# The low halves of the second layer's weights: a negated copy on ScalarE and an adding DMA in place of a subtraction

## The chip, the cores and the metric

One core of a Trainium2 chip runs the kernel. The metric is the device time of one execution in microseconds (us). Names of engines as in the profile: PE is the matrix engine (PEld its weight loads, which overlap it), DVE is VectorE, ACT is ScalarE, POOL is GpSimd, SP is the queue that issues DMAs.

## The reference, cut to what matters

Two layers over 640 tokens (128 prompt tokens and 512 latent tokens), width 1024. Layer 0 is gated attention, layer 1 a bidirectional state-space scan (SSD). The change touches only the two weight matrices of layer 1:

```
proj = h @ w_in            # layer 1: (640 x 1024) @ (1024 x 5184)
z, xbc, dt = split(proj)
xbc = silu(conv3(xbc));  xs, bs, cs = split(xbc)
dt = softplus(dt + bias)
y_f, h_f = scan(xs * dt_f, a_f * dt_f, bs, cs, h0_f)     # chunks of 128 tokens
y_b, h_b = the same, backwards
y = rms_norm((y_f + y_b + d_skip * xs) * silu(z), gnorm_w)
out = x + gate * (y @ w_out)                             # (640 x 2048) @ (2048 x 1024)
```

## The kernel before

**Split operands.** Every large product is computed from fp32 values that are split into a high part (rounded to the reduced type fp32r) and a low part, the value minus its high part. PE then makes three products: high times high, high times low, low times high. A weight tile so exists three times in SBUF: `raw` (as loaded), `wh` (high) and `wl` (low).

**How weights arrive.** `load_split` does it in halves: SP issues the DMA of a raw half (512 KB), ACT copies it to `wh` (line 73, the rounding is the copy's output type), and DVE or POOL subtracts, `wl = raw - wh` (line 74). Which of the two subtracts is set by the list `self.weng`, which is rotated at each half: POOL alone at the start of layer 1, then DVE, POOL, POOL in turn, then DVE alone from the first weights of `w_out` on. All three tiles come from the pool `w`, which has two buffers for each name. So a raw half can be issued when the raw half two places ahead has been read, and a load (two halves) can write its `wh` and `wl` when PE is done with the load two places ahead.

**Stages of layer 1.** (1) 21 loads from `w_in`: 16 of 256 columns for x and z, 4 of 2 x 128 columns for the B and C of a group, and one of 64 columns for dt (a single half of 256 KB). A load of 256 columns serves two units; a unit is 48 matmuls of 322 columns (line 914; lines 1073 for the first z). Between them stand, for each of 4 groups, the scan's steps: POOL masks two decay tiles (lines 1116, 1117) that SP has loaded (line 1112), ACT exponentiates them (1121), POOL adds them (1122), DVE multiplies (1128), PE makes the products. (2) 16 loads from `w_out`, each two rows of 128 of the inner dimension: first 8 for token tiles 2 and 3 (`part_mm`, 24 matmuls of 512 columns a load), the first ones between the steps of the last group's scan, then the same 8 again for token tiles 1, 4 and 0 (36 matmuls a load; line 1368). The output follows at once.

**Order.** Each engine works through its own list in order. A scheduler that builds the kernel decides the order within an engine by a simulated timeline, so an edit can move rows on every engine.

Of the kernel before, what the change touches and what calls it, by code (L numbers as in the profile page):

```python
# [11 lines left out]
ALU = mybir.AluOpType  # L12
# [27 lines left out]
def r32(ap):  # L40
    return ap.bitcast(F32)
# [12 lines left out]
class Hybrid:  # L54
    def __init__(self, tc, A, O, tap=None):
        self.tc, self.nc, self.A, self.O = tc, tc.nc, A, O
        self.tap = tap or {}
        self.n = 0

    def nm(self, s):  # L60
# [15 lines left out]
    def load_split(self, wp, hi, lo, src):  # L76
        k, w = hi.shape[1], hi.shape[2]
        step = max(1, 1024 // w)
        for k0 in range(0, k, step):
            ks = slice(k0, min(k, k0 + step))  # L80
            raw = self.tl(wp, [P, step, w], tag="raw")
            rv = raw[:, 0:ks.stop - k0, :]
            self.nc.sync.dma_start(out=rv, in_=src[:, ks, :])
            self.weng = self.weng[1:] + self.weng[:1]
            self.split(hi[:, ks, :], lo[:, ks, :], rv, self.weng[0])

# [923 lines left out]
    def layer1(self, hT, wp, pj, pa, ctx):  # L1010
        nc, tc, A, O = self.nc, self.tc, self.A, self.O
        sp = self.pool("s1", ctx=ctx)
        self.weng = [nc.gpsimd]
        wk = self.pool("s2", bufs=2, ctx=ctx)
        self.fss = self.tl(self.cp, [P, NT], tag="fss")
        self.one = self.tl(self.cp, [P, 1], tag="one")
# [168 lines left out]
        def lag(f, g, j, before=None):  # L1185
            u = wcur.get("u")
            f(g, j)
            v = wcur["u"]
            if before:
                wcur["u"] = u  # L1190
                before[0](*before[1:])
                wcur["u"] = v
# [8 lines left out]
            self.y_turn(t, g, wk, "u")  # L1201

        def part_mm(k0):
            self.weng = [nc.vector]
            w = self.load_wide(wp, A["l1_w_out"], k0)
            for t in (2, 3):
                if k0 == 0:
                    ps = self.tl(pj, [P, 1024], tag="pj")
                    self.PS[t] = [ps[:, 0:512], ps[:, 512:1024]]
                self.out_mm(t, w, k0)  # L1210
# [7 lines left out]
        next(gen, None)  # L1218
        lag(x_unit, 0, 2, (x_turn, 0, 1))
        next(gen, None)  # L1220
        self.weng = [nc.vector, nc.gpsimd, nc.gpsimd]
        lag(x_unit, 0, 3, (x_turn, 0, 2))
        lag(bc_unit, 0, 0, (x_turn, 0, 3))
        lag(bc_unit, 0, 1, (b_turn, 0))
# [3 lines left out]
        for g in range(NG):  # L1228
# [3 lines left out]
            if last:  # L1232
                pt_ = lambda t, k: (lambda: part_turn(t, k))
                pm_ = lambda k: (lambda: part_mm(k))
                fl = {0: [zf(0), zf(1)], 1: [zf(2)], 2: [zf(3), pt_(2, 0), pt_(3, 0)], 3: [pt_(2, 1), pt_(3, 1), pm_(0)],
                      4: [pt_(2, 2), pt_(3, 2), pm_(2)], 5: [pm_(4)], 6: [pm_(6)], 7: [pm_(8)], 8: [pm_(10)]}
            else:
                fl = {j: [nx(j)] for j in range(4)}
                fl.update({4: ([zf(0)] if g else []) + [lambda: x_turn(g + 1, 3)], 5: [zf(1)] if g else [], 6: [lambda: bc_unit(g + 1, 0)], 7: [lambda: bc_unit(g + 1, 1)], 8: [zf(2), lambda: b_turn(g + 1)], 9: [zf(3)]})
# [59 lines left out]
        for n in range(4, 6):  # L1299
            self.mod_gate(1, n, self.grow[1, n], pa, "a", wk, "xw0", "xw0", 2)  # L1300
        part_mm(12)
        part_mm(14)
        for t in (2, 3):
            self.final_out(t, wk, "u", "ym")
# [160 lines left out]
```

## Time and profile before

| what | value |
|---|---|
| median of 3 runs | 996.82 us (993.96 to 996.9) |
| the profiled execution | 996.55 us, its span 994.8 us |
| granted clock of PE over the span | 0.981 |
| busy: PE, DVE, ACT, POOL | 937.9, 656.3, 515.3, 431.1 us |
| layer 1 begins at about | 430 us of the span |
| DMA: moved, share of the 16 engines | 127.91 MB, 39.6% |

The span is that of the instructions; 1.75 us of the profiled time lie around it. Matmuls overlap, so a PE that is busy for all of a stretch is not at its peak by that alone. A figure in brackets behind a row of the timeline is the engine's idle time ahead of it and what ended it.

### The profile page before, as it was taken

What the parts mean: (1) busy time and instruction counts of PE and PEld (TensorE: products, weight loads), DVE (VectorE), ACT (ScalarE), POOL (GpSimd) and SP (SyncE); (2) the same over time, 40 slices, a digit from 0 to 9 for tenths busy, and PEclk for the clock granted to TensorE, in tenths of its full rate; (3) what the DMA queues carried; (4) which work ended last, traced back from release to release, by engine and by line L of the source; (5) the groups of instructions that cost most, each with busy time, mean ns of one, the idle gap of its engine ahead of it and who ended that gap; (6) DMA issues with size and microseconds to landing.
All of it is one profiled execution on the core that took longest, in us unless ns stands there. A gap on an engine that the chain in (4) does not pass through costs nothing. (4 is left out here: it accounts for less than half of the span.)

```text
span 994.8 us, 17000 instructions
## 1 busy us (share of the span) xinstructions
PE 937.9 (94%) x6466; PEld 835.0 (84%) x6466; DVE 656.3 (66%) x1046; ACT 515.3 (52%) x1212; POOL 431.1 (43%) x415
## 2 busy tenths in 40 slices
PE   5998999999999989989899979999999999989998
PEld 3897879879997789989898878889988898658786
DVE  5468665666675764884759854956587547797663
ACT  5355666757775763433446564446436642554240
POOL 3345235227270162364267475739484853333000
PEclk9999999999999989999999999999999999989999
DMA  9942234221113222333234352344524441455752
GB/s 319 351 128 87 86 127 138 67 73 43 37 49 107 85 93 100 123 106 89 86 131 148 121 181 88 109 139 145 151 87 146 156 133 64 128 183 190 257 194 96
DMA packets 90354, 127.91 MB, mean 129 GB/s; under 512 B 6816, under 2 KB 65312, under 8 KB 90272
## 3 DMA queue, kind: packets, MB, share of 16 engines
q1 hardware_dynamic: 90272, 126.82, 39.6%
q8 instruction: 51, 0.84, 0.3%
q14 instruction: 31, 0.25, 0.1%
HBM read 115.10 MB, written 11.70 MB: 127 GB/s over the span
## 5 line engine op out<-in xcount | busy, mean ns | idle before, releaser
L914 PE MATMUL pj<-h,wh 128*128 128x322 f32 (+1 forms) x1248 | 298.3, 325 | 8.7 <-DVE B L999 7.5
L914 PEld LDWEIGHTS pj<-h,wh 128*128 128x128 f32 (+1 forms) x1248 | 211.2, 189 | 21.5 <-issue 14.0
L74 POOL TENSOR_TENSOR wl<-raw,wh 128x512 fp32r<-128x512 f32 (+1 forms) x70 | 133.1, 1912 | 184.6 <-ACT wh L73 182.9
L914 PE MATMUL pj<-h,wl 128*128 128x322 f32 (+1 forms) x624 | 198.6, 319 | 0.0
L73 ACT CAST wh<-raw 128x1024 fp32r<-128x1024 f32 (+1 forms) x117 | 103.0, 912 | 79.7 <-DMA raw<-in_l_w_out 22.4
L1121 ACT ACTIVATE am<-am,nb 128x128 f32<-128x128 f32 x320 | 97.9, 389 | 62.4 <-POOL am L1117 39.9
L914 PEld LDWEIGHTS pj<-h,wl 128*128 128x128 f32 (+1 forms) x624 | 118.2, 190 | 3.9 <-issue 3.6
L283 PE MATMUL pp<-wh,big 128*128 128x256 f32 x576 | 112.1, 284 | 0.5 <-ACT sg L527 0.5
L283 PEld LDWEIGHTS pp<-wh,big 128*128 128x128 f32 x576 | 91.2, 188 | 0.9 <-ACT sg L527 0.7
L74 DVE TENSOR_TENSOR wl<-raw,wh 128x1024 fp32r<-128x1024 f32 x47 | 62.8, 1347 | 38.0 <-ACT wh L73 38.0
L283 PE MATMUL pp<-wl,big 128*128 128x256 f32 x288 | 81.1, 282 | 0.0
L74 DVE TENSOR_TENSOR pl<-pt,ph 128x512 fp32r<-128x512 f32 (+1 forms) x100 | 59.2, 599 | 25.9 <-ACT ph L73 25.1
L633 DVE TENSOR_REDUCE nm<-S 128x1 f32<-128x640 f32 x64 | 52.3, 819 | 13.7 <-PE S L630 12.7
L73 ACT CAST ph<-pt 128x512 fp32r<-128x512 f32 (+1 forms) x100 | 51.4, 517 | 19.1 <-PE pt L658 14.3
L1122 POOL TENSOR_TENSOR am<-am,am 128x1024 f32<-128x1024 f32 x20 | 48.7, 2437 | 26.2 <-ACT am L1121 26.2
L637 ACT ACTIVATE Pt<-S,nm 128x640 f32<-128x640 f32 x64 | 51.2, 802 | 13.4 <-PE pt L658 9.9
L1368 PE MATMUL pj<-wh,h 128*128 128x512 f32 x160 | 54.4, 413 | 0.5 <-ACT wh L73 0.5
L283 PEld LDWEIGHTS pp<-wl,big 128*128 128x128 f32 x288 | 54.3, 188 | 0.0
L658 PE MATMUL pt<-cst,Pt 128*128 128x128 f32 x320 | 51.6, 279 | 2.6 <-DVE pl L74 2.3
L630 PE MATMUL S<-kT,qT 128*128 128x320 f32 x256 | 51.1, 324 | 2.3 <-ACT Pt L637 2.3
L1116 POOL TENSOR_SCALAR_AFFINE_SELECT am<-am 128x1024 f32<-128x1024 f32 x20 | 24.2, 1211 | 56.6 <-DMA am<-acd 32.3
L658 PEld LDWEIGHTS pt<-cst,Pt 128*128 128x128 f32 x320 | 37.2, 142 | 11.8 <-PE S L630 3.7
(347 smaller groups left out, 2135.9 us busy)
## 6 DMA issues: line engine op xcount, KB each, us to landing
raw<-in_l_w_in SPq DMA_DIRECT2D x48, 512.0 KB
am<-acd SPq DMA_DIRECT2D x40, 512.0 KB
raw<-in_l_w_out SPq DMA_DIRECT2D x36, 512.0 KB
og<-in_l_mod_w SPq DMA_DIRECT2D x29, 512.0 KB
raw<-in_l_w_in SPq DMA_DIRECT2D x25, 256.0 KB
mw<-in_l_mod_w SPq DMA_DIRECT2D x11, 512.0 KB
raw<-in_l_mod_w SPq DMA_DIRECT2D x8, 512.0 KB
yzd<-ys SPq DMA_DIRECT2D x6, 640.0 KB
```

The costliest lines, as they stand in the source:

```text
L73: (heng.tensor_copy if heng else self.nc.scalar.copy)(hi, src)
L74: (eng or self.nc.vector).tensor_tensor(lo, src, r32(hi), op=ALU.subtract)
L283: nc.tensor.matmul(ps, a[:, k, cs], b[:, k, :], start=k == 0 and a is hi and b is w[0], stop=k == KD - 1 and a is lo)
L630: nc.tensor.matmul(S[:, 192 + 320 * q:512 + 320 * q], qTs[g, t][:, h, :], kT[:, hl, 320 * q:320 * q + 320], start=hl == 0, stop=hl == 1)
L633: nc.vector.tensor_reduce(c["m"], c["s"], axis=AX.X, op=ALU.max, negate=True)
L637: nc.scalar.activation(Pt, c["s"], AF.Exp, bias=c["m"], scale=1.0, accum_out=rss[g][t][:, h:h + 1])
L658: nc.tensor.transpose(pt[:, 2 * i + j, :], Pts[j][:, kt * P:kt * P + P], self.ident)
L914: nc.tensor.matmul(ps[0:m, 190 + 322 * half:512 + 322 * half], w[b][:, k, off:off + m], hT[s][:, k, 322 * half:322 * half + 322], start=fi ...
L1116: nc.gpsimd.affine_select(out=af[0], in_=af[0], pattern=[[0, 8], [1, P]], base=0, channel_multiplier=-1, compare_op=ALU.is_ge, fill=NEG)
L1121: nc.scalar.activation(af[d][:, h, :], af[d][:, h, :], AF.Exp, bias=self.nb[:, t, i:i + 1], scale=1.0)
L1122: nc.gpsimd.tensor_tensor(af[0], af[0], af[1], op=ALU.add)
L1368: nc.tensor.matmul(self.PS[t][n], y[a][:, kk, :], b, start=k0 + k == 0 and i == 0, stop=k0 + k == 15 and i == 2)
```

## The change

In layer 1 (a flag, `added`), `load_split` no longer subtracts. ACT makes the high part as before and then writes its negative into `wl` (fp32 view of `wh`, times -1). POOL issues a DMA that reads the same raw weights from DRAM a second time and adds them to what stands in `wl`. The list `weng` is no longer set in layer 1. Layer 0 is as it was.

```
@@ class Hybrid
+        self.added = False
@@ load_split
             self.nc.sync.dma_start(out=rv, in_=src[:, ks, :])
+            if self.added:
+                self.nc.scalar.copy(hi[:, ks, :], rv)
+                self.nc.scalar.mul(lo[:, ks, :], r32(hi[:, ks, :]), -1.0)
+                self.nc.gpsimd.dma_start(out=lo[:, ks, :], in_=src[:, ks, :], accum_op=ALU.add)
+                continue
             self.weng = self.weng[1:] + self.weng[:1]
             self.split(hi[:, ks, :], lo[:, ks, :], rv, self.weng[0])
@@ layer1
-        self.weng = [nc.gpsimd]
+        self.added = True
@@ part_mm
-            self.weng = [nc.vector]
@@ layer1, after the third step of dt_stage
-        self.weng = [nc.vector, nc.gpsimd, nc.gpsimd]
```

Line numbers of the kernel after are 6 higher from `rstd` on, 5 from `part_mm` and 4 behind it; lines 86, 87 and 88 are the copy, the negation and the adding DMA. The order that the builder gives shows three places.

On ACT, at the end of the program, the last three loads from `w_out` before (`raw` with its numbers is one half):

```order
L73 CAST wh_1963_10964<-raw_1964_10965 128x1024
L73 CAST h10_1958_10950<-u_1960_10955 128x512
L73 CAST h10_1958_10950<-u_1961_10959 128x512
L73 CAST wh_1963_10964<-raw_1965_10969 128x1024
L73 CAST wh_1967_11010<-raw_1968_11011 128x1024
L73 CAST wh_1967_11010<-raw_1969_11015 128x1024
L73 CAST wh_1971_11020<-raw_1972_11021 128x1024
L73 CAST wh_1971_11020<-raw_1973_11025 128x1024
```

and the same three loads in the kernel after:

```order
L86 CAST wh_1963_11031<-raw_1964_11032 128x1024
L86 CAST wh_1963_11031<-raw_1965_11037 128x1024
L87 ACTIVATE wl_1962_11030<-wh_1963_11031 128x1024 x2
L86 CAST wh_1967_11079<-raw_1968_11080 128x1024
L86 CAST wh_1967_11079<-raw_1969_11085 128x1024
L87 ACTIVATE wl_1966_11078<-wh_1967_11079 128x1024 x2
L86 CAST wh_1971_11091<-raw_1972_11092 128x1024
L86 CAST wh_1971_11091<-raw_1973_11097 128x1024
L87 ACTIVATE wl_1970_11090<-wh_1971_11091 128x1024 x2
```

A load has four ACT instructions where it had two, and both negations stand behind both copies.

On POOL, in the last group's scan, where the first loads of `w_out` come in (`am0`, `am1` are the decay tiles), before:

```order
L1117 AFFINE_SELECT am1_1800_10002<-am1_1800_10002 128x1024
L1116 AFFINE_SELECT am0_1799_10001<-am0_1799_10001 128x1024
L1122 TENSOR_TENSOR am0_1799_10001<-am0_1799_10001,am1_1800_10002 128x1024
L1116 AFFINE_SELECT am0_1819_10148<-am0_1819_10148 128x1024
L1117 AFFINE_SELECT am1_1820_10149<-am1_1820_10149 128x1024
L1122 TENSOR_TENSOR am0_1819_10148<-am0_1819_10148,am1_1820_10149 128x1024
```

and after:

```order
L1123 AFFINE_SELECT am1_1800_10043<-am1_1800_10043 128x1024
L88 DMA wl_1840_10313<-in_l1_w_out 128x1024 x2
L1122 AFFINE_SELECT am0_1799_10042<-am0_1799_10042 128x1024
L1128 TENSOR_TENSOR am0_1799_10042<-am0_1799_10042,am1_1800_10043 128x1024
L88 DMA wl_1855_10400<-in_l1_w_out 128x1024
L1122 AFFINE_SELECT am0_1819_10189<-am0_1819_10189 128x1024
L88 DMA wl_1855_10400<-in_l1_w_out 128x1024
L1123 AFFINE_SELECT am1_1820_10190<-am1_1820_10190 128x1024
L88 DMA wl_1865_10460<-in_l1_w_out 128x1024
```

The adding DMAs of `w_out` stand in POOL's list between the masks, where POOL had no weights to work on; DVE had them.

On PE, the start of the last load but two (`pj` and `a` are the accumulators; `B0`, `B1`, `C0`, `C1` and `T` are parts of y), before:

```order
L1368 MATMUL pj_1916_10674<-wh_1963_10964,B0_1941_10837 128x512
L1368 MATMUL pj_1916_10674<-wl_1962_10963,B0_1941_10837 128x512
L1368 MATMUL pj_1916_10674<-wh_1963_10964,B1_1942_10838 128x512
L1368 MATMUL pj_1916_10674<-wh_1963_10964,B0_1941_10837 128x512
L1368 MATMUL pj_1917_10675<-wh_1963_10964,C0_1944_10844 128x512
L1368 MATMUL pj_1916_10674<-wl_1962_10963,B0_1941_10837 128x512
```

and after:

```order
L1372 MATMUL pj_1916_10731<-wh_1963_11031,B0_1941_10900 128x512
L1372 MATMUL pj_1917_10732<-wh_1963_11031,C0_1944_10907 128x512
L1372 MATMUL a_1918_10733<-wh_1963_11031,T_1947_10914 128x512
L1372 MATMUL a_1919_10734<-wh_1963_11031,T_1947_10914 128x512
L1372 MATMUL pj_1916_10731<-wl_1962_11030,B0_1941_10900 128x512
L1372 MATMUL pj_1916_10731<-wh_1963_11031,B1_1942_10901 128x512
```

The first product that needs a low half stood second in a load; now it stands fifth, behind four products of the high half.

## Rows read from the trace of the kernel before

**Rows 1.** The page, part 1: busy time of each engine.

```profile
PE 937.9 (94%) x6466; PEld 835.0 (84%) x6466; DVE 656.3 (66%) x1046; ACT 515.3 (52%) x1212; POOL 431.1 (43%) x415
```

**Rows 2.** Busy time by stretch of the span (us), granted clock, DMA share, GB/s.

```profile
core 0: us, PE busy (x) PEld busy (x) DVE busy (x) ACT busy (x) POOL busy (x), PEclk, DMA share, GB/s
445.00:845.00 400.00, 384.23 (x2557) 350.17 (x2558) 258.43 (x314) 197.37 (x475) 227.18 (x155) 0.99 0.40 124
845.00:895.00 50.00, 43.06 (x207) 31.75 (x206) 42.57 (x49) 26.77 (x58) 17.80 (x14) 0.90 0.49 153
895.00:982.00 87.00, 86.74 (x396) 70.00 (x395) 54.25 (x67) 32.61 (x39) 7.68 (x15) 1.00 0.58 194
```

**Rows 3.** Chain that ended last, near 900: start, length, what.

```profile
897.64 3.93 DMA raw<-in_l_w_out
...
901.60 1.05 ACT wh L73
...
902.68 1.22 DVE wl L74
...
909.92 3.36 DMA raw<-in_l_w_out
```

**Rows 4.** Groups by shape, from 425 us to the end: busy, mean ns, idle before.

```profile
L74 POOL TENSOR_TENSOR wl<-raw,wh 128x1024 fp32r<-128x1024 f32 x29 | 73.8, 2556 | 47.3 <-ACT wh L73 45.8 <-issue 1.5
L73 ACT CAST wh<-raw 128x1024 fp32r<-128x1024 f32 x72 | 72.9, 1045 | 63.4 <-DMA raw<-in_l_w_out 22.2 <-PE pj L914 19.2 <-PE a L1368 11.7
L74 DVE TENSOR_TENSOR wl<-raw,wh 128x1024 fp32r<-128x1024 f32 x43 | 58.0, 1358 | 37.8 <-ACT wh L73 37.8
```

**Rows 5.** The page, part 3: the DMA queues.

```profile
q1 hardware_dynamic: 90272, 126.82, 39.6%
```

**Rows 6.** SP's issues of raw halves (line 83): ns min/median/max.

```profile
L83 SPq DMA_DIRECT2D raw<-in_l_w_out x32: 327/332/445, 812.3 to 969.1; - x32
```

**Rows 7.** Subtractions on DVE from 895 to 982 us.

```profile
L74 DVE TENSOR_TENSOR wl<-raw,wh 128x1024 fp32r<-128x1024 f32 x23 | 27.8, 1221 | 17.2 <-ACT wh L73 17.2
```

**Rows 8.** Timeline of ACT, 963 to 980 us: start, length, what.

```profile
965.66 2.00 ACT L73 CAST wh<-raw 128x1024 fp32r<-128x1024 f32 x2 [4.39 <-PE a L1368]
973.90 2.01 ACT L73 CAST wh<-raw 128x1024 fp32r<-128x1024 f32 x2 [6.24 <-PE a L1368]
```

**Rows 9.** Timeline of DVE, 963 to 980 us.

```profile
966.74 2.36 DVE L74 TENSOR_TENSOR wl<-raw,wh 128x1024 fp32r<-128x1024 f32 x2 [4.12 <-ACT wh L73]
```

**Rows 10.** Timeline of ACT, 457 to 460 us: the load of the first unit of x.

```profile
457.46 2.00 ACT L73 CAST wh<-raw 128x1024 fp32r<-128x1024 f32 x2 [2.12 <-PE a L1073]
459.36 0.43 ACT L1057 ACTIVATE zs<-a 128x320 f32<-128x320 f32 x1
```

**Rows 11.** Timeline of POOL, 458 us.

```profile
458.59 4.75 POOL L74 TENSOR_TENSOR wl<-raw,wh 128x1024 fp32r<-128x1024 f32 x2 [9.93 <-ACT wh L73]
```

**Rows 12.** Timeline of PE, 461 us: first low product of the first unit of x.

```profile
461.06 0.40 PE L914 MATMUL pj<-h,wl 128*128 128x322 f32 x1
```

**Rows 13.** Busy time by stretch, behind that place; columns as in rows 2.

```profile
455.00:475.00 20.00, 20.00 (x138) 19.36 (x137) 10.44 (x14) 5.94 (x8) 9.57 (x4) 1.00 0.38 106
475.00:480.00 5.00, 2.66 (x19) 2.40 (x18) 4.96 (x8) 3.27 (x5) 1.63 (x1) 0.96 0.01 2
```

**Rows 14.** Timeline of ACT, 652 to 682 us: copies of two loads in turn.

```profile
654.85 2.00 ACT L73 CAST wh<-raw 128x1024 fp32r<-128x1024 f32 x2 [0.90 <-PE pj L914]
...
678.54 1.99 ACT L73 CAST wh<-raw 128x1024 fp32r<-128x1024 f32 x2
```

**Rows 15.** Who waited for line 74 on PE's side with a weight's low half (us, times).

```profile
  PEld pj L1368: 2.7, 4
```

**Rows 16.** Timeline of DVE, 873 us.

```profile
872.95 3.24 DVE L74 TENSOR_TENSOR wl<-raw,wh 128x1024 fp32r<-128x1024 f32 x2
```

**Rows 17.** Timeline of ACT, 867 us.

```profile
867.12 2.00 ACT L73 CAST wh<-raw 128x1024 fp32r<-128x1024 f32 x2
```

**Rows 18.** POOL's groups from 445 to 845 us.

```profile
L74 POOL TENSOR_TENSOR wl<-raw,wh 128x1024 fp32r<-128x1024 f32 x27 | 68.6, 2554 | 47.3 <-ACT wh L73 45.8 <-issue 1.5
```

## The prediction

> **What bounds the kernel now.** I read the page's busy times first, then the stretches of layer 1, the chain that ended last, the groups by shape, and at last single places of the timelines. PE is busy for 937.9 of 994.8 us [rows 1], so time can be won only where PE waits, and lost wherever a new wait reaches it. The stretches show three parts [rows 2]. From 445 to 845 us (the loads of `w_in` and the scan) PE waits 15.8 of 400 us, with every other engine under two thirds busy and the DMA engines at 0.40. From 845 to 895 (the last group's scan, with the first loads of `w_out`) PE waits 6.9 of 50 us, DVE is busy for 42.6, and the granted clock is 0.90. From 895 to 982 (the rest of `w_out`) PE is busy for 86.74 of 87 us at full clock, while the DMA engines stand at 0.58 and move 194 GB/s. The chain there runs raw DMA, copy, subtraction, and then the next raw DMA [rows 3]: a supply that is just fast enough.
>
> **How close the supply is.** At the end a load's two copies are released by PE at 965.66 and the next two at 973.90 [rows 8]. So a load of three token tiles lasts 8.24 us on PE, 0.229 us for each of its 36 matmuls. The copies take 2.00 us together, and the subtractions are done at 966.74 + 2.36 = 969.10, 3.4 us after the release [rows 9]. PE needs that low half 8.24 us after the release. A new way of making it therefore has some 5 us more.
>
> **What goes.** In layer 1, 29 wide subtractions on POOL (73.8 us) and 43 on DVE (58.0 us) [rows 4], among them the 23 DVE ones of the last stage [rows 7].
>
> **What comes on ACT.** 73 negations of the shape of a copy. I price each as a copy, 1.045 us [rows 4]. The last stage gets 23 x 1.045 = 24 us on top of 32.6, of 87; the middle gets the other 50, 52 us at most on top of 197.4, of 400 [rows 2]. ACT bounds neither; 0 by itself. Its delay counts in the latency below: both copies stand ahead of both negations, so after a release the negations end at 3.0 and 4.0 us.
>
> **What comes on POOL: the issue.** The trace has no DMA with data from POOL: one queue carries 126.82 of the 127.91 MB [rows 5]. The issue costs at least what SP needs for a raw half, 0.33 us [rows 6], and I bound it above by the work that it replaces, 2.56 us [rows 4]. I take 1 us, nearer to the row that is also an issue.
>
> **What comes on the DMA engines.** 524 KB per half are read once more and added to what stands in SBUF. No row shows a DMA that adds. The lower bound is a plain copy. The last stage moves 194 GB/s at a share of 0.58 [rows 2], which is 334 GB/s at full share, so a copy costs 0.524 MB / 334 GB/s = 1.57 us of all 16 engines. The upper bound is 3.13 us, if reading the destination costs as much as another copy. I take the middle, 2.35 us: a copy is a read and a write, an add is two reads and a write, three halves of it.
>
> The Trainium skill speaks against this change here. In "Collectives: The Full Stack", section "The bandwidth ceiling: the fold count and why AG ≠ RS ≠ AR", it says that a reduction by DMA pays nothing for the addition but runs at half the rate of a copy, since its two source reads go through the same ring. By that rule the price would be the 3.13 us of the upper bound and the last stage would grow by 35.5 us in place of the 17.5 us below. No row of this trace shows it, since nothing here adds by DMA.
>
> **Last stage, 895 to 982.** The present traffic keeps the engines busy for 0.58 x 87 = 50.5 us [rows 2]. Adding 23 halves [rows 7] at 2.35 us gives 54.0 us more, 104.5 us of work for 87 us: **+17.5 us**. At 1.57 us it is 86.6 us, which just fits, +0; at 3.13 us it is 122.5 us, +35.5. The stretch ahead of it cannot work far ahead: its 32 - 23 = 9 halves [rows 6, 7] at 2.35 us and the 0.49 x 50 = 24.5 us of old traffic fill 45.6 of 50 us, and two buffers let a load be written only when PE has finished the load two ahead.
>
> **Latency in the same stage.** A raw half lands 3.36 to 3.93 us after its start [rows 3]. An adding one I put at 3.6 + (2.35 - 1.57) = 4.4 us, with 3.4 (no dearer than the fastest raw) and 3.93 + 1.57 = 5.5 us as bounds. After the release: 3.0 for the first negation, 4.0 for the second, 1.0 for the issue, 4.4 to land, that is 8.4 and 9.4 us. PE wants the first at 8.24 + 4 x 0.229 = 9.2 us, because four high products now stand ahead of the first low one, and the second half a load later. So three tiles are just in time, with no reserve. A load of two tiles has 24 matmuls, 5.5 us; a low half at 8.4 against 5.5 + 0.5 (two high products) is 2.4 us late, and with two loads in flight about half of it, 1.2 us, is lost per load. Some four such loads lie behind 895, 5 us. That lies in the same time as the engines' excess and is not added to it. It goes into the range.
>
> **Start of layer 1.** The first unit of x has no load ahead of it. Copies end at 459.46, an activation of z stands behind them until 459.79 [rows 10], the negation ends near 460.8; with issue and landing the low half is there at 460.8 + 1.0 + 4.4 = 466.2. Before, POOL began its subtractions at 458.59 [rows 11], and PE took the first low product at 461.06, the third matmul of the unit [rows 12]. That is a wait of 5.1 us. PE is full from 455 to 475 but idle for 2.3 us from 475 to 480, with DVE at 4.96 of 5 [rows 13]: those 2.3 us may take up part of it. Between 2.8 and 5.1, I take **+4 us**. Bounds of issue and landing move it by about 2 us either way.
>
> **The middle, 445 to 845.** Copies of two loads stand at 654.85 and 678.54, 24 us apart [rows 14], and PE waited for no low half there; in all it waited 2.7 us for four of them, in line 1368 alone [rows 15]. A low half after 9.4 us has cover of more than 10 us, and old and new traffic are 160 + 41 x 2.35 = 256 of 400 us. So 0. POOL gives back 68.6 us of subtractions [rows 18] for 41 issues. Without this cover each load would lose what the start loses.
>
> **Relief of DVE.** In 845 to 895 the copies of one load begin at 867.12 [rows 17], but DVE gets to its subtractions only at 872.95 and ends them at 876.19 [rows 16]. An adding DMA would be there at 867.12 + 3.0 + 1.0 + 4.4 = 875.5, 0.7 us sooner: too little to count with the DMA engines as full as they then are, so 0.
>
> **Sum.** 996.55 + 17.5 + 4 = **1018 us**, against the profiled execution, which stands 0.3 us under the median of 996.82.
>
> **Rivals.**
> - *Double price.* The add reads its destination at the full cost of a copy: +35.5 + 4, 1036 us. For it: the destination has to be read by somebody, and no engine but the DMA's is named. Against it: nothing in the trace shows reads to be the limit rather than writes. It decides if the added half costs over 2.7 us (halfway).
> - *Hidden.* The add costs no more than a copy: 86.6 of 87 us fit, and 4 us of the start stay, about 1001 us; 997 if the idle 2.3 us and more take up the start, and 1005 with the two-tile loads' 5 us. For it: the DMA share of 0.58 leaves 0.42. Against it: this would need engines full without a gap.
> - *Faster.* DVE loses nine wide subtractions, at 1.36 us each some 12 of its 42.6 us in 845 to 895 [rows 2, 4], and PE waits 6.9 us there. If issue and landing take the lower bounds, the low half of 867.12 lands at 867.12 + 3.0 + 0.3 + 3.4 = 873.8, 2.4 us ahead of the subtraction's end. At most all of PE's 6.9 us come back: 989.6 us. It decides if issue and landing together stay near these 3.7 us and a half costs the engines no more than 1.57 us, so that the last stage fits as well. Against it: a landing of 3.4 us with twice the traffic.
> - *POOL held.* If an issue occupies POOL for as long as two subtractions, 5.1 us, then POOL has 227.2 - 68.6 + 41 x 5.1 = 368 of 400 us [rows 2, 18], masks come late, and each `w_out` half adds 4 us of latency to a load that has no reserve: about +20 over the forecast, 1038 us. Against it: SP's 0.33 us.
>
> **How the numbers follow.** This kernel's measurement tells about 0.3%, 3 us, from no change. Chances: forecast 0.42 (its own range 1010 to 1028, from a price of 2.0 to 2.8 us per half), double price 0.25, hidden 0.13, faster 0.11, POOL held 0.09. The hidden case falls half within 0.3%. So faster 0.11, same 0.06, slower 0.83. The range leaves out the faster case and the lower half of the hidden one and begins at 999. Above it goes past 1036 to 1052: 5 us for two-tile loads, 2 for the start, 3 for the nine halves ahead (24.5 + 9 x 3.13 = 52.7 of 50), and the rest for a clock that falls when PE waits, as it does to 0.90 from 845 to 895.
>
> **What the changed profile would show.** Last stage: DMA share near 1.0, PE waiting at the low products of line 1372 for a DMA into `wl`, and some 17 us more for the same matmuls. If the share stays well under 0.9 while PE waits, latency or the issue is what costs, not the engines. POOL's DMA rows show the issue (1 us; 0.33 and 2.56 the bounds), and the time from issue to landing shows the 4.4 us. At the first unit of x the third matmul should begin near 466 in place of 461. The middle should be as long as before, with POOL less busy by 68.6 - 41 = 28 us. The prediction is wrong if an added half costs the engines as little as a copy, if POOL's issue takes several us, or if PE waits for low halves in the middle, where I see 10 us of cover.

## The result, and the profile after

The changed kernel takes 1052.24 us (median of 4 runs, 1050.99 to 1053.81) against 996.86: a ratio of 1.0561 (95% interval 1.0534 to 1.0589). It is slower, by 55 us, where 21.5 were forecast.

The page of the changed kernel, its busy times (answer to [rows 1]), its two data queues ([rows 5]), POOL's groups of adding DMAs (busy, mean ns), and their landing (median us from issue):

```profile
PE 955.7 (91%) x6466; PEld 849.1 (81%) x6466; DVE 597.7 (57%) x1003; ACT 583.4 (56%) x1285; POOL 432.1 (41%) x458
...
q1 hardware_dynamic: 90272, 126.82, 37.4%
q0 software_dynamic: 30864, 38.02, 22.7%
...
L88 POOL DMA_DIRECT2D wl<-in_l_w_in x41 | 56.6, 1504 | 74.2 <-ACT wl L87 72.8
...
L88 POOL DMA_DIRECT2D wl<-in_l_w_out x32 | 28.3, 900 | 93.5 <-ACT wl L87 92.3
...
wl<-in_l_w_in POOLq DMA_DIRECT2D x40, 512.0 KB, 8.5
wl<-in_l_w_out POOLq DMA_DIRECT2D x32, 512.0 KB, 8.6
```

DVE loses 58 us of work, POOL 74 and gains 85 of issues. PE does the same 6466 matmuls in 17.8 us more busy time. A low half lands 8.5 us after its issue began; a raw one took 3.4 to 3.9 us [rows 3].

Busy time by stretch, columns as in [rows 2]:

```profile
445.00:845.00 400.00, 380.58 (x2514) 349.93 (x2513) 233.56 (x289) 231.28 (x505) 206.26 (x166) 0.97 0.75 173
...
895.00:950.00 55.00, 41.88 (x178) 32.74 (x174) 21.56 (x33) 31.23 (x46) 19.00 (x31) 0.81 0.87 213
950.00:1000.00 50.00, 41.87 (x146) 31.96 (x147) 12.85 (x19) 21.10 (x24) 8.64 (x10) 0.84 1.02 289
```

Where DMA stood at 0.58 and PE never waited, DMA now stands at 0.87 to 1.02, PE is busy for 84 of 105 us, and its granted clock, a mean between the levels 1.2 and 2.4 GHz, is 0.81 to 0.84 in place of 1.00.

The next table says where the time goes. It compares the start of the same PE product in two traces: the number is that start minus the start in the kernel before, in us. Places: the 25th, 145th and last product of line 914 (after: 920), the 97th of line 1368 (after: 1372), the end of the last product, the end of the span. In the three ring runs the 97th is another product of the same part. Each row is one profiled execution; that of e7 is the fastest of its runs, 5 us under their median.

| run | 25th (450.4) | 145th (478.8) | last of `w_in` (848.1) | 97th of `w_out` (896.2) | PE's end (990.2) | span (994.8) |
|---|---|---|---|---|---|---|
| changed kernel | 13.5 | 11.5 | 13.4 | 22.9 | 50.6 | 54.3 |
| e1, `w_in` only | 12.6 | 10.6 | 10.6 | 8.9 | 11.5 | 11.5 |
| e2, `w_out` only | -0.4 | -0.5 | 0.7 | 13.1 | 37.6 | 41.1 |
| e3, plain copy | 11.2 | 8.8 | -0.1 | 2.6 | 12.4 | 16.2 |
| e4, half of each add | 2.1 | 8.2 | 2.7 | 6.6 | 15.7 | 19.1 |
| e5, negation on DVE | 6.4 | 13.0 | 21.5 | 29.7 | 62.7 | 65.8 |
| e6, half of each raw load | 12.4 | 10.6 | 12.6 | 16.6 | 38.3 | 42.1 |
| e7, last two loads subtracted | 11.9 | 9.7 | 11.1 | 20.0 | 47.5 | 47.6 |
| e8, middle only | 0.0 | 0.0 | -0.3 | -2.9 | -0.4 | -0.4 |
| e9, ring of five, adding | 13.6 | 11.8 | 11.1 | 19.7 | 42.8 | 43.1 |
| e10, ring, plain copy | 11.8 | 9.2 | 1.1 | 1.5 | 9.3 | 9.6 |
| e11, ring, subtraction | -0.5 | -0.4 | 1.1 | -5.0 | 1.1 | 1.1 |

So there are four losses: 13.4 us up to the end of `w_in`, nearly all at its first loads; 9.5 us beside the last group's scan; 27.7 us in the rest of `w_out`; and 3.7 us behind PE's last product.

**The start.** PE's first low product of layer 1, then POOL's rows for the load that it waits for, of the changed kernel (start, length, what, idle before):

```profile
443.88 0.64 PE L1079 MATMUL a<-h,wl 128*128 128x322 f32 x1 [9.48 <-DMA wl<-in_l_w_in]
...
434.46 1.51 POOL L88 DMA_DIRECT2D wl<-in_l_w_in  x1 [2.11 <-ACT wl L87]
...
436.48 1.83 POOL L88 DMA_DIRECT2D wl<-in_l_w_in  x1
437.30 2.46 POOL L258 TENSOR_TENSOR hm<-hm,shift 128x512 f32<-128x512 f32 x1
```

The load that comes too late is the one for z, ahead of the first unit of x: PE waits 9.48 us. In the kernel before, POOL subtracted there at 432.07. The unit of x adds its own wait behind it. The products around these waits are slower too: the granted clock from 432 to 455 us is 0.78, before it was 0.93.

**The end.** From the chain that ended last in the changed kernel, one wait of a three-tile load from the release on, and a raw load further on:

```profile
941.07 0.05 ACT wh L86
941.11 0.91 issue
942.02 1.05 ACT wh L86
943.07 0.96 ACT wl L87
944.04 0.28 issue
944.32 6.33 DMA wl<-in_l_w_out
...
950.69 2.93 PE pj L1372 x6
...
971.03 13.59 DMA raw<-in_l_w_out
```

The low half is there 9.6 us after the release. The second piece tells more: from its issue on, a raw load took 13.59 us, with nothing in its path but the other transfers. It landed in 3.93 us before [rows 3].

Who waited for the low tiles (us, times), from 425 us to the end, and the time from issue to landing:

```profile
  PE pj L1372: 20.6, 9
...
DMA to landing us min/median/max: 5.2/8.5/13.0
```

PE lost 20.6 us in line 1372 to these waits. They do not make up the whole loss, as the last two parts show, each from and to the same products (848.1 to 896.2 to 990.2 before, 861.5 to 919.1 to 1040.8 after; columns as in [rows 2]), first before and then after:

```profile
848.10:896.20 48.10, 41.16 (x197) 29.85 (x196) 41.40 (x50) 27.34 (x58) 15.40 (x13) 0.89 0.51 162
896.20:990.20 94.00, 93.72 (x421) 75.23 (x419) 59.10 (x75) 32.04 (x38) 7.92 (x16) 1.00 0.55 185
```

```profile
861.50:919.10 57.60, 45.12 (x218) 33.72 (x217) 34.87 (x51) 36.62 (x70) 21.16 (x25) 0.82 0.79 215
919.10:1040.80 121.70, 104.70 (x399) 80.92 (x397) 26.00 (x43) 50.72 (x56) 22.35 (x32) 0.89 0.89 229
```

What PE waited for in each part of the changed kernel (total, times, longest):

```profile
PE pj L1372 <- DMA wl<-in_l_w_out: 3.8, 2, 3.3
PE a L1141 <- DVE am L1134: 3.2, 1, 3.2
PE a L1377 <- POOL ssq L1104: 3.0, 1, 3.0
PE pj L1372 <- ACT h L74: 2.5, 1, 2.5
```

```profile
PE pj L1372 <- DMA wl<-in_l_w_out: 16.8, 7, 3.6
```

In the rest of `w_out` PE is idle for 17.0 us (0.3 before), all at low halves, and its products take 104.7 us in place of 93.7: the loss of 27.7 us is 16.7 of waits and 11.0 of slower products, at a granted clock of 0.89 in place of 1.00. Beside the last group's scan PE is idle for 12.5 us (6.9 before). Only 3.8 of them are at low halves; the others are at steps of the scan and of y on DVE, POOL and ACT. The DMA share is 0.79 there, so the engines are not full on average. By which way the scan's steps came late is not shown.

### The profile page after: what moved, and what is told of

It is laid out like the page before. It is cut to its first block, busy times and chain, and to the rows that moved or that the text cites. A ratio compares the mean times of both kernels' runs of the same rounds, so it can differ in the third digit from the quotient of the medians.

```text
span 1049.1 us, 17087 instructions
## 1 busy us (share of the span) xinstructions
PE 955.7 (91%) x6466; PEld 849.1 (81%) x6466; DVE 597.7 (57%) x1003; ACT 583.4 (56%) x1285; POOL 432.1 (41%) x458
## 4 chain that ended last, share of the span: by engine, by line
PE 62%; DMA 13%; DVE 7%; ACT 7%; issue 5%; POOL 4%; SPq 0%; POOLq 0%; DVEq 0%; ACTq 0%
PE pj L920 19%; PE pp L289 8%; PE pj L1372 5%; DMA wl<-in_l_w_out 4%; PE po L674 3%; DMA am<-acd 3%; PE acc L385 3%; PE a L847 3%; PE pt L664 3%; PE S L636 3%; ACT am L1127 2%; DMA wl<-in_l_w_in 2%; DMA raw<-in_l_w_out 2%; PE pp L181 2%; ACT wh L86 2%
## 5 line engine op out<-in xcount | busy, mean ns | idle before, releaser
L920 PEld LDWEIGHTS pj<-h,wh 128*128 128x128 f32 (+1 forms) x1248 | 213.8, 191 | 19.6 <-issue 10.3
L86 ACT CAST wh<-raw 128x1024 fp32r<-128x1024 f32 (+1 forms) x73 | 73.3, 1038 | 76.6 <-PE pj L1372 33.6
L75 POOL TENSOR_TENSOR wl<-raw,wh 128x512 fp32r<-128x512 f32 (+1 forms) x40 | 58.0, 1460 | 136.3 <-ACT wh L74 136.1
L88 POOL DMA_DIRECT2D wl<-in_l_w_in x41 | 56.6, 1504 | 74.2 <-ACT wl L87 72.8
L87 ACT ACTIVATE wl<-wh 128x1024 fp32r<-128x1024 f32 (+1 forms) x73 | 73.9, 1045 | 0.1
L88 POOL DMA_DIRECT2D wl<-in_l_w_out x32 | 28.3, 900 | 93.5 <-ACT wl L87 92.3
L639 DVE TENSOR_REDUCE nm<-S 128x1 f32<-128x640 f32 x64 | 52.4, 820 | 13.5 <-PE S L636 12.7
L1372 PE MATMUL pj<-wh,h 128*128 128x512 f32 x160 | 56.5, 434 | 2.5 <-ACT h L74 2.5
```

What stands on the lines that cost most here:

```text
L75: (eng or self.nc.vector).tensor_tensor(lo, src, r32(hi), op=ALU.subtract)
L86: self.nc.scalar.copy(hi[:, ks, :], rv)
L87: self.nc.scalar.mul(lo[:, ks, :], r32(hi[:, ks, :]), -1.0)
L88: self.nc.gpsimd.dma_start(out=lo[:, ks, :], in_=src[:, ks, :], accum_op=ALU.add)
L639: nc.vector.tensor_reduce(c["m"], c["s"], axis=AX.X, op=ALU.max, negate=True)
L920: nc.tensor.matmul(ps[0:m, 190 + 322 * half:512 + 322 * half], w[b][:, k, off:off + m], hT[s][:, k, 322 * half:322 * half + 322], start=fi ...
```

## The experiments

The edits are against the changed kernel. The first four tell the parts and the price apart.

**e1 and e2: one matrix each.**

```
@@ part_mm (e1)
+            self.added = False
+            self.weng = [nc.vector]
@@ layer1, part_mm (e2: w_in as in the kernel before)
-        self.added = True
+        self.weng = [nc.gpsimd]      # and the later rotation, as before
@@ part_mm
+            self.added = True
```

> Adding DMAs for the loads of w_in only; the loads of w_out go back to copy and subtraction on DVE. The changed kernel's PE is 11 to 13 us behind the kernel before when the w_in products end and 50 us behind at the end. If start and end are separate losses: about 997 + 13 = 1010 us, with the DMA engines near 0.58 in the last stage again and PE's waits there gone. If adding anywhere disturbs the whole (POOL's order, DMA queues), clearly more than 1015. If the loss of the start is made good later: under 1003.

> The reverse: w_in with subtractions on POOL and DVE as in the kernel before, adding DMAs for the loads of w_out only. If start and end are separate losses: 997 + 39 = 1036 us, and the end is as in the changed kernel (DMA share about 1.0 in its fullest 50 us). If the end suffers only because it starts from a late w_in stage: under 1020.

e1: 1011.01 us, ratio 1.0165 (1.0132 to 1.0198). e2: 1036.82 us, 1.0421 (1.0389 to 1.0453). In medians 16.2 and 42.0 us, 58 together against 55: start and end are separate losses. In e1 the last stage is as it was, DMA 0.64 and 0.43, while e2 fills it (first two rows e1, then e2):

```profile
895.00:950.00 55.00, 50.56 (x231) 40.30 (x232) 38.73 (x50) 19.96 (x25) 14.63 (x20) 0.97 0.64 215
950.00:1000.00 50.00, 50.00 (x219) 40.53 (x218) 28.80 (x36) 16.11 (x20) 0.00 (x0) 1.00 0.43 148
```

```profile
895.00:950.00 55.00, 43.06 (x170) 33.23 (x170) 16.93 (x27) 24.98 (x30) 15.90 (x28) 0.81 0.93 230
950.00:1000.00 50.00, 41.80 (x167) 32.14 (x168) 14.72 (x22) 22.85 (x27) 8.64 (x10) 0.97 0.97 280
```

**e3: copy in place of add. e4: half of each add.**

```
@@ load_split (e3)
-  self.nc.gpsimd.dma_start(out=lo[:, ks, :], in_=src[:, ks, :], accum_op=ALU.add)
+  self.nc.gpsimd.dma_start(out=lo[:, ks, :], in_=src[:, ks, :])
@@ load_split (e4)
+  self.nc.gpsimd.dma_start(out=lo[:, ks, :w // 2], in_=src[:, ks, :w // 2], accum_op=ALU.add)
```

> As the changed kernel, but POOL's DMA copies the raw weights into the low tile and does not add (the low part is then the raw weight, so the addition is left out). Order, issue and waits are the same. If the addition is what doubles a packet's time (107 ns for 1 KB and 353 ns for 4 KB on POOL's queue, against about 54 and 190 on SP's): packets of POOL's queue take 54 and 190 ns, landing falls from 8.5 to 5 or 6 us, the last stage fits again, and the time is 1000 to 1012 us. If POOL's queue itself is the slow part: packets and time as in the changed kernel, 1045 to 1055 us.

> As the changed kernel, but the adding DMA covers only the first half of the columns (the other half of the low part keeps the negated high part; half of the additions are left out). Issues, negations and waits are as many as before. If the DMA engines' time is the bound of the last stage: 50.5 + 23 x 1.4 = 83 of 87 us fit, the last stage loses 0 to 5 us, and the time is 1003 to 1013 us. If the latency from the release of a buffer to the landing is the bound: a landing shorter by 1.5 to 3 us leaves 10 us or more of loss in the w_out loads, 1018 to 1030 us.

e3: 1011.42 us, 1.0161 (1.0123 to 1.0199). e4: 1016.11 us, 1.0223 (1.0194 to 1.0253). The queues from 895 to 985 us (packets, MB, share of 90 us), first of the changed kernel, then of e3:

```profile
q0 software_dynamic: 2312, 8.40, 50.6%
q1 hardware_dynamic: 5428, 12.88, 41.0%
```

```profile
q1 hardware_dynamic: 5939, 16.13, 52.1%
q0 software_dynamic: 2965, 10.81, 36.1%
```

This is the price that no row of before had. Adding: 0.506 x 90 us / 8.40 MB x 0.524 MB = 2.84 us for a half. Copying on the same queue: 0.361 x 90 / 10.81 x 0.524 = 1.58 us. So for these 4 KB runs POOL's queue costs next to nothing extra (the forecast's copy was 1.57), and the addition makes the packets 1.8 times as long. The halves of `w_in` come in shorter runs (1 KB, for B and C 512 B). With the addition the page of e1 gives 14.5% of 1006.3 us for 21.24 MB, 3.60 us per half; e3 has, from 430 to 826 us (share of 396 us):

```profile
q0 software_dynamic: 26256, 21.24, 27.4%
```

That is 2.68 us per half without the addition: here it is 1.3 times, and the queue itself is the dearer part.

The order that the builder gives e3 is that of the changed kernel on every engine. With the addition left out, landing falls to 3.6/5.9/9.7 us (minimum, median, maximum) and the time by 41 us, into the first range expected. e4 lies between its two, and its order is another one, so it decides little. And e3 and e4 change the engines' time and the landing together, so they don't tell these apart; each still loses 12 to 13 us between the end of `w_in` and PE's end.

**e5 and e6: the latency alone, and the traffic alone.**

```
@@ load_split (e5)
-  self.nc.scalar.mul(lo[:, ks, :], r32(hi[:, ks, :]), -1.0)
+  self.nc.vector.tensor_scalar(out=lo[:, ks, :], in0=r32(hi[:, ks, :]), scalar1=-1.0, scalar2=None, op0=ALU.mult)
@@ load_split (e6)
+  hw = w // 2 if self.added and w == D else w
+  self.nc.sync.dma_start(out=rv[:, :, 0:hw], in_=src[:, ks, 0:hw])
...
+  for c in range(0, w, hw):
+      self.nc.scalar.copy(hi[:, ks, c:c + hw], rv[:, :, 0:hw])
```

> As the changed kernel, but DVE writes the negated high part in place of ACT, so that a half can be negated while ACT copies the next one: the low half can start 1 to 2 us sooner after a release, with the same DMA traffic. If the latency from release to landing sets the loss of the w_out loads, each of the 16 loads gives back 0.5 to 1 us: 1036 to 1044 us. If the DMA engines' time sets it: 1048 to 1055 us, with their share near 1.0 as before.

> As the changed kernel, but of each raw half of w_out only the first 512 columns are loaded, and the high part is copied from them twice (the high parts of the other 512 columns are thus of wrong weights). Adding DMAs, negations and their order of release stay. The last stage loses 23 x 0.8 = 18 us of DMA work. If the DMA engines' time is the bound: 15 to 20 us faster than the changed kernel, 1032 to 1037 us. If the latency is the bound, and the adding DMA itself is what is late: 0 to 6 us faster, 1046 to 1052 us.

e5: 1064.08 us, 1.0707 (1.0651 to 1.0763), slower than either expectation. The negation took 0.69 us in place of 1.05 and mostly began with the end of its copy, yet from the end of `w_in` to PE's end e5 lost 41.2 us against 37.2. What it lost more in `w_in` (21.5 against 13.4) was not followed up: the builder's order is another one there, and the negations stand in DVE's list between the scan's steps. So e5 does not decide between the two. e6: 1038.85 us, 1.0447 (1.0400 to 1.0495), 13 us less than the changed kernel, with the adding DMAs as many and as large. That is 2 us short of the range for the engines' time and far from the one for the latency. From issue to landing a low half in `w_out` took 7.0 us in place of 8.6, so raw loads beside it decide how fast it comes. But the raw load is also the first link of the low half's own chain, so e6 alone does not exclude the latency.

**e9, e10, e11: twice the cover.** A ring of five rows replaces the two pairs of buffers. The core of the edit:

```
@@ load_row, in place of load_wide
+  big = [[self.tl(wp, [P, 2, D], F32R, tag=g) for g in ("wl", "wh")] for _ in range(2)]
+  self.ring = [[x[:, i:i + 1] for x in b] for b in big for i in range(2)]
+  self.ring.append([self.tl(self.w3, [P, 1, D], F32R, tag=g) for g in ("wl", "wh")])
...
+  self.load_split(wp, hi, lo, src.rearrange("(k p) n -> p k n", p=P)[:, k0:k0 + 1, :])
@@ part_mm and the loop over k0: for each of the two rows of a load
+  w = self.load_row(wp, A["l1_w_out"], k)
+  for t in rest:
+      self.out_mm(t, w, k, 1)
```

> As the changed kernel, but a load of w_out is one row of 128 (one half) in a ring of five low and five high tiles in place of two pairs: a row is used four rows after its tile came free (4 x 4.1 = 16.5 us with three token tiles, 4 x 2.75 = 11 us with two) in place of one load (8.2 and 5.5 us). DMA traffic is the same. If the latency from release to landing (10 to 11 us in the changed kernel) sets the loss of the w_out loads: nearly all of it goes, 1010 to 1020 us. If the DMA engines' time sets it (50.5 + 23 x 2.79 = 114.7 us of work in 87): the last stage still loses 25 us or more, 1033 to 1045 us, with the DMA share near 1.0.

> The ring of five rows with a plain copy on POOL's queue in place of the adding DMA (the addition is left out). The two-load kernel with the plain copy stood at 1011 us and lost 12.5 us in the w_out loads and 3.8 behind PE's last matmul, while its DMA work (50.5 + 23 x 1.58 = 86.8 us) just fits. If that loss is latency: it goes with the ring, 996 to 1002 us. If it is the DMA engines' time, or another price of the queue: 1006 to 1013 us.

> The control: the kernel before (copy and subtraction) with the ring of five rows. The ring by itself should cost nothing: 993 to 999 us. If smaller loads cost something of their own (order, more waits), that number is to be taken off the two ring runs with DMAs.

e11, the control: 995.96 us, 0.9998 (0.9982 to 1.0013): the ring by itself costs nothing. e9: 1040.09 us, 1.0439 (1.0407 to 1.0470). e10: 1006.23 us, 1.0084 (1.0056 to 1.0111). The stretches of e9:

```profile
895.00:950.00 55.00, 43.51 (x190) 33.18 (x189) 22.43 (x33) 33.40 (x46) 22.14 (x34) 0.91 0.95 247
950.00:1000.00 50.00, 37.59 (x138) 27.68 (x137) 11.84 (x18) 21.69 (x24) 6.90 (x8) 0.90 0.95 265
```

With twice the room between release and use, the end still loses 31.7 us (from 11.1 to 42.8), at a DMA share of 0.95. The engines' time is the bound of the last stage; latency was worth at most 37.2 - 31.7 = 5.5 us of it. PE's waits for low halves from the 97th product on fell from 16.8 to 9.7 us, and a wait of 6.1 us came instead for a part of y whose own transfer took 17.47 us. Raw loads, which have two buffers in e9 as before, are 46% of the chain that ended last from 940 to 1000 us. More buffers for them were not tried; with the engines at 0.92 of the 117.1 us from the 97th product to PE's end, they could give back some 9 us at most, by estimate. The ring puts PE's last products back accumulator by accumulator too, and the stretch behind them is 4.9 us. e10 says that latency was part of the plain copy's loss: 12.5 us became 8.2. It didn't go wholly: the time lies at the lower end of the second expectation. The DMA share in 895 to 950 is 0.99 and from 950 to 1000 0.64, so "just fits" on average is no fit in each half of the stage.

**e7: the last two loads subtracted on DVE.**

```
@@ ahead of the last two loads
+        self.added, self.weng = False, [nc.vector]
         w = [self.load_wide(wp, A["l1_w_out"], k0) for k0 in (12, 14)]
```

> As the changed kernel, but the last two loads of w_out are made by copy and subtraction on DVE, which puts PE's last 72 matmuls back accumulator by accumulator. In the changed kernel all four accumulators end in the last few us: from PE's last matmul to the end 8.3 us, against 4.6 in the kernel before. If that order is what the end costs: the stretch behind PE's last matmul is 4.6 us again, and with the waits of two loads less (2 to 6 us) 1040 to 1047 us. If the stretch is long for another reason, it stays at 8 us.

e7: 1049.41 us, 1.0537 (1.0490 to 1.0584), an interval that overlaps the changed kernel's and a time above the 1040 to 1047 that were expected: the total does not show the gain. The profile is clearer: DVE's last steps, in the kernel before, in the changed one and in e7 (first and last of eight rows in each):

```profile
983.94 1.41 DVE L1389 SCALAR_TENSOR_TENSOR ym<-pj,fss,xt 128x512 f32<-128x512 f32 x2 [6.60 <-PE pj L1368]
...
991.00 0.69 DVE L1390 TENSOR_TENSOR ym<-ym,am 128x512 f32<-128x512 f32 x1
```

```profile
1038.13 1.41 DVE L1393 SCALAR_TENSOR_TENSOR ym<-pj,fss,xt 128x512 f32<-128x512 f32 x2 [32.77 <-PE pj L1372]
...
1044.61 0.97 DVE L1394 TENSOR_TENSOR ym<-ym,am 128x512 f32<-128x512 f32 x1
```

```profile
1031.47 1.41 DVE L1394 SCALAR_TENSOR_TENSOR ym<-pj,fss,xt 128x512 f32<-128x512 f32 x2 [6.57 <-issue]
...
1038.54 0.69 DVE L1395 TENSOR_TENSOR ym<-ym,am 128x512 f32<-128x512 f32 x1
```

Before, the accumulators end one after another, and DVE works on the first 6 us ahead of PE's end at 990.2. After, PE goes round the four of them and ends them nearly together, the last at 1040.8; DVE's steps of 7.5 us begin only at 1038.13, and most of them stand behind. In e7 the stretch behind PE's end is 4.7 us again.

**e8: only where a low half has time.** `added` is set from the fourth unit of x to the last load of `w_in`; ahead of it POOL subtracts, behind it DVE.

> Adding DMAs only where a low half has time: w_in from the fourth unit of x on; ahead of it POOL subtracts, and behind it (w_out) DVE, as in the kernel before. If the loss of the w_in part is only that of its first loads: 994 to 1000 us, no change from the kernel before. If the loads in the middle lose too, or the issues hold POOL's masks: 1003 us or more. If POOL's and DVE's relief is worth something: under 992.

e8: 997.84 us, 1.0024 (1.0000 to 1.0048), no difference that this kernel's measurement can tell. Its 34 adding halves, from 445 to 845 us:

```profile
445.00:845.00 400.00, 383.79 (x2559) 350.88 (x2560) 243.25 (x303) 229.09 (x509) 213.93 (x166) 0.99 0.71 169
```

PE is as busy as before (384.23 [rows 2]) with DMA at 0.71. But that balance has two sides. What PE waited for from 495 to 845 us (total, times, longest), first the two largest in the kernel before, then e8, then e3, whose order is that of the changed kernel:

```profile
PE pj L914 <- DVE B L999: 7.5, 2, 5.2
PE a L1138 <- DVE ys L1175: 1.8, 3, 1.0
```

```profile
PE pj L920 <- DVE B L1005: 5.6, 1, 5.6
PE a L1141 <- ACT wh L86: 3.4, 2, 2.0
PE pj L920 <- DMA wl<-in_l_w_in: 3.3, 3, 1.6
```

```profile
PE pj L920 <- DVE B L1005: 5.4, 2, 5.0
PE pj L920 <- ACT Wh L987: 1.7, 1, 1.7
```

For these DVE steps PE waited 9.3 us before and 5.6 us in e8, which starts as early: the relief of DVE is there. With the addition there are waits of 3.3 us for low halves and of 3.4 us that are put down to ACT's copy; with the plain copy there are none. They take the relief again. In the table e3 makes good 9 us of its late start between the 145th product and the last of `w_in`, and the changed kernel nothing. How much of these 9 us is relief, and how much only that a late PE finds its other inputs ready, no run tells apart.

## Why the prediction was wrong, point by point

- **Price of an added half: right mechanism, too small.** The step was "I take the middle, 2.35 us". It is 2.84. With that the sum's own formula, 50.5 + 23 x 2.84 = 115.8 of 87, gives +28.8; the trace shows 27.7. The forecast had 17.5. That the formula then comes so near is in part luck: it lets the engines be full all the time, where they stood at 0.89, and it has no term for the slower products, 11.0 of the 27.7 us. By its own condition (over 2.7 us) the double-price rival holds, and its 1036 us was the nearer number. The rule of the Trainium skill ("Collectives: The Full Stack", "The bandwidth ceiling: the fold count and why AG ≠ RS ≠ AR") said half the rate of a copy; e3 against the changed kernel shows 1.58 against 2.84, 1.8 times, and 1.3 times in `w_in`. The rule pointed the right way; whether the second read is the reason, no run here shows.
- **845 to 895: "45.6 of 50 us", taken as no loss.** 9.5 us were lost there, and without the addition (e3) 2.7. The engines were not full (0.79), so a higher price alone does not explain it: PE waited 3.8 us for low halves and longer than before for the scan's steps. That a sum below the stretch means no loss was the wrong step; e10 too had DMA work for 86.8 of 87 us in the last stage and still lost time.
- **Start: the step "The first unit of x has no load ahead of it" looked at the wrong load.** The load of z comes first and has no cover either; PE waited 9.48 us for it. From the start of the issue to the landing it took 9.37 us there and 8.5 in the median, where the forecast had 1.0 and 4.4, so the start cost 11 to 13 us in place of 4.
- **Latency in the last stage.** The release-to-landing time of three tiles was 9.6 us in the wait shown (forecast 8.4). That it lies in the same time as the engines' excess held: e9 took 5.5 us away and the engines kept the rest.
- **The order of PE's last products was read as a help alone.** The text counted four high products ahead of the first low one as cover. The same reordering moved all ends to the last few us: 3.7 us, a term that the sum did not have.
- **Clock.** It stood only in the range. PE's busy time rose by 17.8 us for the same matmuls, so a third of the 54 us is slower products beside waits; the stretches with waits show 0.81 to 0.84.
- **The middle: right in the sum, not in its parts.** It cost 2 us in the changed kernel and nothing in e8. But PE did wait for low halves there (2.3 us in the changed kernel, 3.3 in e8), where the text saw 10 us of cover, and in e8 shorter waits for DVE paid for it. The DMA share came out at 0.75, not 0.64, since a half of `w_in` cost 3.60 us.
- **The rivals.** Hidden is refuted by the price. Of the faster rival the relief is there (some 4 us less waiting for DVE in e8, in the middle rather than from 845 to 895), but the addition takes it again; e8 kept the change to the loads with cover and came out even. POOL held: the issues took 0.9 and 1.5 us, not 5.

## What to carry to other kernels

Price a DMA that adds at nearly two copies of its bytes (1.8 in the 4 KB runs here), a copy on POOL's queue in short runs by a row of its own, and ask of each stage whether its DMA engines have that room, not of the kernel's mean (40% here, 58% in the stage that decided). Then walk through the loads at a stage's start, where nothing covers the latency, and take the first of them, not the one that the code names first. When a dependence gets later, read what the builder does to the order at the end: work that finished piece by piece may come to finish all at once.

## What the runs showed of the hardware

- An addition by DMA made a half of 4 KB runs 1.8 times as dear as a copy on the same queue (2.84 and 1.58 us of all engines), a half of `w_in` 1.3 times (3.60 and 2.68 us), and lengthened POOL's issue too: 900 ns against 546 in `w_out`, 1504 against 812 in `w_in`.
- A POOL operation can run while POOL's issue lasts, by the rows of the profile: the tensor operation at 437.30 begins inside the issue of 436.48 that takes 1.83 us.
- Transfers on SP's queue and POOL's share the engines: with an adding stream beside it one raw load of 512 KB took 13.59 us in place of 3.4 to 3.9.
